# A hybrid encoder block on one core: the two channel chunks of a group take turns through the long convolution, v is split two steps later, and the tap rows move to the queue of the weights

## The chip, the cores and the metric

One core of a Trainium2 chip runs the whole block as one program. The metric is the device time of one execution in microseconds; a version's time is the median of its timed runs. A profiled execution (the trace) is a run of its own.

## The reference

One layer on x of 256 x 2048 float32. `w_in` makes q, k, v, r, gate inputs, the convolution branch's input u and two merge gates. One branch is gated linear attention (GLA), the other ("Hyena") is a short convolution followed by two long ones with gates. Both are projected, merged by sigmoid gates, projected again, and followed by layer norm and a squared-ReLU MLP with layer norm. The change is in the Hyena branch:

```python
uc = _short_conv(u, conv_w, conv_b)          # 3 taps along the sequence, per channel, plus bias
v, x1, x2 = jnp.split(uc, 3, axis=-1)
z = v
for o, gate in enumerate((x1, x2)):
    zf = jnp.fft.rfft(z, n=2 * L, axis=1)
    zc = jnp.fft.irfft(zf * filt_f[None, :, o], n=2 * L, axis=1)[:, :L]
    z = gate * (zc + skip[o] * z)
```

## The kernel before

**Products and weights.** Every large product is made of three matmuls of reduced float32: the operand's high part (a rounding copy on ScalarE, ACT, line 84) and low part (a subtraction on VectorE, DVE, line 85) are multiplied as high x high, high x low and low x high. Weights come in 300 blocks of 1 MB: `fetch` (92) loads a block into one of three `raw` buffers on SyncE's queue (SP), two blocks ahead of its use, and splits it in two halves `whi`, `wlo`, each with three buffers. TensorE (PE) thus needs a fresh `whi` from ACT and a fresh `wlo` from DVE for every half block. `token_group` (208) computes 512 output columns for all 256 tokens from four blocks, 24 matmuls each (lines 204 to 206), into two PSUM tiles, one for each 128 tokens.

**Steps.** After each block `pump` advances a clock. `later(d, fn)` puts a piece of side work on the list for d steps later; pieces that fall on the same step run in the order in which they were registered. So side work is interleaved with weight blocks at a granularity of one block. All of this is the order in which the program is written; a scheduler then places the instructions of each engine from it and from its own estimate of when each can start, so that one may move ahead of another. Each engine executes its list strictly in order, GpSimd (POOL) and SP with their DMAs too.

**The stage of the change.** Four times (s = 0 to 3) it runs the token groups v, x1, x2 (`u` columns) and `go` (GLA's output projection): 16 blocks a turn. Each of the first three is followed by `short_conv` (704): DVE multiplies the PSUM with three tap rows into `past`, `ahead` and `y` (line 708: six products of 128 x 512) and adds the bias row (709). Then four DMAs on POOL add `past`, shifted down one token, and `ahead`, shifted up one token, to `y` (716; two large ones of 508 KB and two of one row). They add to the same `y`, so each large one waits for the other. `past`, `ahead` and the four tap rows exist once (`conv_sb`): the next group overwrites them. `load_taps` (701) loads the next tap rows, a broadcast of one row to 128 partitions (1 MB).

**The long convolution.** `hy_v` splits v into `vh` and `vl`. For each 256-channel chunk c of the two in a group, and each order o: `hy_fwd` (732) loads the filter's transform `Tl` and makes two forward transforms on PE (`Zp`, six matmuls), which ACT copies to `Z`; `hy_mul` (745) multiplies on DVE (`Z` sum, `pa`, `pb`, two combinations, one more sum) and splits the result (`Yh`, `Yl`); `hy_inv` (765) transforms back (`yp`, six matmuls), multiplies with the gate x1 or x2 (`zf`) and either splits the result for o = 1 (`zh`, `zl`) or transposes it (`yT`) and stores it. Counted from the end of the v group, hy_v is at step 3; chunk 0 is at steps 5 (forward, product), 9 (inverse), 10, 14; chunk 1 at 13, 17, 18, 22. The buffers `Tl`, `Z`, `pa`, `pb`, `zh`, `zl` exist once. `reload` (824) later reads stored results back into buffers that are free by then.

Of the kernel before, what the change touches and what calls it, by code (L numbers as in the profile page):

```python
# [9 lines left out]
F32 = mybir.dt.float32  # L10
# [6 lines left out]
P = 128  # L17
D = 2048
L = 256
NT = L // P  # L20
# [22 lines left out]
def block_kernel(  # L43
# [24 lines left out]
    nc = tc.nc  # L68
    MM = nc.tensor.matmul
# [43 lines left out]
    def later(d, fn):  # L113
        clock[1] += 1
        side.append((clock[0] + d, clock[1], fn))
# [215 lines left out]

    nc.vector.memset(ones_sb, 1.0)

    def mm3(ps, lh, ll, rh, rl, start, stop):
        MM(ps, lh, rl, start=start, stop=False)
        MM(ps, lh, rh, start=False, stop=False)
        MM(ps, ll, rh, start=False, stop=stop)

# [360 lines left out]
    past, ahead = (conv_sb[:, 2 + i].rearrange("p (t d) -> p t d", t=NT) for i in range(2))  # L699

    def load_taps(i):
        nc.gpsimd.dma_start(conv_sb[:, 0:2].rearrange("p a b -> p (a b)"), conv_rows[i:i + 1, :].broadcast_to([P, 2048]))

    def short_conv(pss, i, tag, name):
        y = hp.tile([P, NT, 512], F32, tag=tag, name=name)
        for tb in range(NT):
            for j, dst in ((0, past), (2, ahead), (1, y)):
                nc.vector.tensor_tensor(dst[:, tb], pss[tb], taps[:, j], op=ALU.mult)
        nc.vector.tensor_tensor(y, y, taps[:, 3:4].broadcast_to([P, NT, 512]), op=ALU.add)
        for dst, src in (  # L710
            (y[1:P], past[0:P - 1]),
            (y[0:1, 1], past[P - 1:P, 0]),
            (y[0:P - 1], ahead[1:P]),
            (y[P - 1:P, 0], ahead[0:1, 1]),
        ):
            nc.gpsimd.dma_start(dst, src, accum_op=ALU.add)
        if i + 1 < 12:
            load_taps(i + 1)
        return y

    def hy_v(s):
        def run():
            z = tuple(hp.tile([P, NT, 512], F32R, tag=t, name=f"{t}{s}") for t in ("vh", "vl"))
            split_hi_lo(z[0], z[1], cst.pop(("v", s)))
            for i in range(2):
                cst[("z", 2 * s + i, 0)] = tuple(t[:, :, i * CW:(i + 1) * CW] for t in z)
        return run
# [1 line left out]
    def gate_part(n, c):  # L729
        return cst[(n, c // 2)][:, :, c % 2 * CW:(c % 2 + 1) * CW]  # L730

    def hy_fwd(c, o):
        def run():
            t = hp.tile([P, 2, 3, CW], F32, tag="Tl", name=f"Tl{c}{o}")
            nc.gpsimd.dma_start(t, T_dram[(c, o)])
            zh, zl = cst.pop(("z", c, o))
            z = hp.tile([P, 3, 2, CW], F32, tag="Z", name=f"Z{c}{o}")
            for ri in range(2):
                pz = psum_side(f"Zp{c}{o}{ri}")
                mm3(pz.rearrange("p (a b) -> p a b", a=2), dfth[:, ri], dftl[:, ri], zh, zl, True, True)  # L740
                nc.scalar.copy(z[:, 2:0:-1, ri, :], pz.rearrange("p (a b) -> p a b", a=2))
            cst[("Z", c, o)] = (t, z)
        return run

    def hy_mul(c, o):
        def run():
            t, z = cst.pop(("Z", c, o))
            a = hp.tile([P, 3, 2, CW], F32, tag="pa", name=f"pa{c}{o}")
            b = hp.tile([P, 3, 2, CW], F32, tag="pb", name=f"pb{c}{o}")
            TT = nc.vector.tensor_tensor  # L750
            full = [P, 3, 2, CW]
            TT(z[:, 0], z[:, 1], z[:, 2], op=ALU.add)
            TT(a, z, t[:, 0, :, None, :].broadcast_to(full), op=ALU.mult)
            TT(b, z[:, :, ::-1, :], t[:, 1, :, None, :].broadcast_to(full), op=ALU.mult)
            TT(a[:, :, 0], a[:, :, 0], b[:, :, 0], op=ALU.subtract)
            TT(a[:, :, 1], a[:, :, 1], b[:, :, 1], op=ALU.add)
            y = a[:, 1:3]
            TT(y, y, a[:, 0:1].broadcast_to([P, 2, 2, CW]), op=ALU.add)
            yh = hp.tile([P, 2, 2, CW], F32R, tag="pb", name=f"Yh{c}{o}")
            yl = hp.tile([P, 2, 2, CW], F32R, tag="Yl", name=f"Yl{c}{o}")  # L760
            split_hi_lo(yh, yl, y)
            cst[("Y", c, o)] = (yh, yl)
        return run

    def hy_inv(c, o):
        def run():
            yh, yl = cst.pop(("Y", c, o))
            py = psum_side(f"yp{c}{o}")
            py3 = py.rearrange("p (a b) -> p a b", a=2)
            mm3(py3, dfth[:, 2], dftl[:, 2], yh[:, :, 0], yl[:, :, 0], True, False)  # L770
            mm3(py3, dfth[:, 3], dftl[:, 3], yh[:, :, 1], yl[:, :, 1], False, True)
            zf = hp.tile([P, NT, CW], F32, tag="zf", name=f"zf{c}{o}")
            nc.vector.tensor_tensor(zf, py3, gate_part(("x1", "x2")[o], c), op=ALU.mult)
# [31 lines left out]
    for s in range(NCH // 2):  # L805
        for k, n in enumerate(("v", "x1", "x2")):
            pss = token_group(xT, f"u{n}{s}")
            cst[(n, s)] = short_conv(pss, 3 * s + k, n, f"c{n}{s}")
            if k == 0:
                later(3, hy_v(s))  # L810
                for i in range(2):
                    c, d = 2 * s + i, 5 + 8 * i
                    later(d, hy_fwd(c, 0))
                    later(d, hy_mul(c, 0))
                    later(d + 4, hy_inv(c, 0))
                    later(d + 5, hy_fwd(c, 1))
                    later(d + 5, hy_mul(c, 1))
                    later(d + 9, hy_inv(c, 1))
        gla_o_group()


# [1 line left out]

    def reload(c):
        def run():
            yr = hp.tile([P, 2, L], F32, tag=("v", "x1")[c % 2], name=f"yr{c}")
            nc.gpsimd.dma_start(yr, yh_dram[c])
            split_hi_lo(yhT[:, 2 * c:2 * c + 2, 0], yhT[:, 2 * c:2 * c + 2, 1], yr)
        return run
# [421 lines left out]
```

## Time and profile before

| | |
|---|---|
| timed runs | 1901.42, 1903.06, 1907.38 us; median 1903.06 |
| the profiled execution | 1907.28 us, its span (first to last instruction) 1905.3 us |
| busy | PE 1853.6, PEld 1553.2, DVE 1284.3, ACT 893.8, POOL 76.2 us |
| mean granted PE clock | 0.987 |
| weight loads | 300 of 1 MB; 399 MB in all, 210 GB/s over the span |
| first `v` product to last `go` product | 457.5 to about 909 us |

PEld is PE's weight load, which overlaps the matmuls. In a waits row, "PE go L205 <- DVE wlo L85: 24.6, 4, 7.6" means that PE stood idle ahead of line 205 until DVE's line 85 was done, for 24.6 us in total, 4 times, at most 7.6 us. In a time line, a row has start, duration, engine, line, operation and, in brackets, the idle time before it and what ended it. DMA rows tell the time from issue to landing.

### The profile page before, as it was taken

The numbers are of one execution on the slowest core, as the hardware profiler recorded it, in microseconds if no ns is written. First come the engines' busy times: TensorE is split into PE (matmuls) and PEld (weight loads), VectorE is DVE, ScalarE is ACT, GpSimd is POOL, SyncE is SP. The second block draws the span as 40 slices with busy tenths as digits, with TensorE's granted clock in tenths as the row PEclk, the third lists the DMA queues.
The fourth block names the chain that finished last, engine by engine and source line by source line (L and its number), as shares of the span: only waits on it lengthen the run. The fifth ranks groups of instructions, "written<-read, shape, count | busy, mean of one in ns | idle before, by whom it ended". The sixth has DMA issues, their size and how long they took to land.

```text
span 1905.3 us, 22925 instructions
## 1 busy us (share of the span) xinstructions
PE 1853.6 (97%) x8999; PEld 1553.2 (82%) x8999; DVE 1284.3 (67%) x1578; ACT 893.8 (47%) x1160; POOL 76.2 (4%) x116
## 2 busy tenths in 40 slices
PE   9999999999999898888999999999999999999999
PEld 7888888888777686666888889888888888888887
DVE  6878968664777786777865667666545655565557
ACT  6555658764344343333544445444434443444332
POOL 0000000000101101111000000000000000000000
PEclk9999999999999999988999999999999999999999
DMA  8667755345787877777655574555555545555553
GB/s 318 219 234 279 256 208 188 133 169 211 224 275 226 228 233 221 230 217 220 229 190 197 179 296 177 199 209 190 188 189 197 196 180 199 199 178 198 191 186 131
DMA packets 65117, 399.43 MB, mean 210 GB/s; under 512 B 8009, under 2 KB 10457, under 8 KB 24305
## 3 DMA queue, kind: packets, MB, share of 16 engines
q1 hardware_dynamic: 46080, 324.03, 47.2%
q0 software_dynamic: 11872, 54.14, 10.5%
q10 hardware_dynamic: 7056, 19.80, 2.9%
q8 instruction: 71, 1.16, 0.2%
q14 instruction: 38, 0.30, 0.0%
HBM read 369.15 MB, written 16.25 MB: 202 GB/s over the span
## 4 chain that ended last, share of the span: by engine, by line
PE 76%; DMA 8%; DVE 7%; issue 6%; ACT 1%; POOL 1%; SPq 0%; DVEq 0%; POOLq 0%; ACTq 0%
PE f L145 12%; PE f L149 6%; PE w L205 6%; PE w L206 6%; PE w L204 6%; DMA cx<-conv_sb 4%; DMA cv<-conv_sb 4%; PE g L205 3%; PE g L206 3%; PE g L204 3%; DVE wlo L85 2%; PE ho L205 2%; PE ho L204 2%; PE ho L206 2%; PE go L205 1%
## 5 line engine op out<-in xcount | busy, mean ns | idle before, releaser
L85 DVE TENSOR_TENSOR wlo<-raw,whi 128x1024 fp32r<-128x1024 f32 x584 | 711.4, 1222 | 373.7 <-ACT whi L84 371.8
L84 ACT CAST whi<-raw 128x1024 fp32r<-128x1024 f32 x584 | 614.1, 1055 | 599.4 <-PE w L206 187.9
L145 PE MATMUL f<-hT,whi 128*128 128x512 f32 x984 | 235.1, 391 | 0.0
L145 PEld LDWEIGHTS f<-hT,whi 128*128 128x128 f32 x984 | 180.8, 188 | 35.0
L205 PE MATMUL w<-wlo,f 128*128 128x512 f32 x480 | 186.7, 389 | 0.0
L206 PE MATMUL w<-whi,f 128*128 128x512 f32 x480 | 186.7, 389 | 0.0
L204 PE MATMUL w<-whi,f 128*128 128x512 f32 x480 | 167.4, 389 | 0.0
L149 PEld LDWEIGHTS f<-hT,wlo 128*128 128x128 f32 x984 | 126.2, 191 | 4.8
L149 PE MATMUL f<-hT,wlo 128*128 128x256 f32 x984 | 127.7, 283 | 0.0
L205 PE MATMUL ux<-wlo,xT 128*128 128x512 f32 x256 | 103.5, 404 | 7.3 <-DVE wlo L85 7.1
L204 PEld LDWEIGHTS w<-whi,f 128*128 128x128 f32 x480 | 90.1, 188 | 18.7
L205 PEld LDWEIGHTS w<-wlo,f 128*128 128x128 f32 x480 | 90.1, 188 | 18.7
L206 PEld LDWEIGHTS w<-whi,f 128*128 128x128 f32 x480 | 90.1, 188 | 18.6
L206 PE MATMUL ux<-whi,xT 128*128 128x512 f32 x256 | 101.9, 398 | 0.0
L157 ACT ACTIVATE f_l<-f 128x256 f32<-128x256 f32 x64 | 24.7, 385 | 162.1 <-PE f L145 159.3
L205 PE MATMUL g<-wlo,xT 128*128 128x512 f32 x256 | 100.1, 391 | 0.7 <-DVE wlo L85 0.7
L206 PE MATMUL g<-whi,xT 128*128 128x512 f32 x256 | 99.8, 390 | 0.0
L158 DVE SCALAR_TENSOR_TENSOR f_s<-f,f_l 128x256 f32<-128x256 f32 x64 | 27.2, 425 | 105.2 <-ACT f_l L157 105.2
L204 PE MATMUL ux<-whi,xT 128*128 128x512 f32 x256 | 92.6, 396 | 4.6 <-ACT whi L84 2.9
L204 PE MATMUL g<-whi,xT 128*128 128x512 f32 x256 | 93.1, 390 | 0.0
L205 PE MATMUL go<-wlo,yg 128*128 128x512 f32 x128 | 53.8, 421 | 24.6 <-DVE wlo L85 24.6
L205 PEld LDWEIGHTS ux<-wlo,xT 128*128 128x128 f32 x256 | 49.4, 193 | 22.9 <-DVE wlo L85 12.8
(431 smaller groups left out, 3232.1 us busy)
## 6 DMA issues: line engine op xcount, KB each, us to landing
raw<-wblk SPq DMA_DIRECT2D x300, 1024.0 KB, 4.8
Td<-T POOLq DMA_DIRECT2D x16, 768.0 KB, 5.0
conv_sb<-conv_rows POOLq DMA_DIRECT2D x12, 1024.0 KB, 13.0
Tl<-Td POOLq DMA_DIRECT2D x16, 768.0 KB, 4.8
w<-w4s ACTq DMA_DIRECT2D x16, 512.0 KB, 4.9
cx<-conv_sb POOLq DMA_DIRECT2D x16, 508.0 KB, 8.2
xw<-first SPq DMA_DIRECT2D x5, 896.0 KB, 12.9
zr<-ln_rows ACTq DMA_DIRECT2D x4, 1024.0 KB, 9.3
```

The source lines that it names most:

```text
L84: return (nc.scalar.copy(hi, src), nc.vector.tensor_tensor(lo, src, hi.bitcast(F32), op=ALU.subtract))
L85: nc.vector.tensor_tensor(lo, src, hi.bitcast(F32), op=ALU.subtract))
L145: MM(ps[:, :, ts], hi[:, js], act[:, kt, :, ts], start=(kt == 0 and opens), stop=(kt == KT - 1))
L149: MM(ps[:, 0, ts], lo[:, js], act[:, kt, 0, ts], start=False, stop=False)
L157: nc.scalar.activation(low, ps[:, 1], AF.Copy, scale=scale)
L158: nc.vector.scalar_tensor_tensor(dst, ps[:, 0], scale, low, op0=ALU.mult, op1=ALU.add)
L204: MM(pss[tb], sh, wh, start=(kt == 0), stop=False)
L205: MM(pss[tb], sh, wl, start=False, stop=False)
L206: MM(pss[tb], sl, wh, start=False, stop=(kt == KT - 1))
```

## The change

- The two chunks of a group alternate, one every four blocks: (chunk 0, o = 0), (chunk 1, o = 0), (chunk 0, o = 1), (chunk 1, o = 1) at steps 7, 11, 15, 19 for forward transform and product, and four steps later for the inverse. On a common step the order is forward, inverse of the one before, product.
- `hy_v` is at step 5 instead of 3.
- `Tl` is loaded in a step of its own, one step ahead of the transform.
- `hold`: the first matmul of each forward transform keeps its written place among PE's instructions.
- `load_taps` is issued on SP, the queue of the weights, two steps after the convolution, instead of on POOL at once.
- The short convolution's six products go by tap (past, y, ahead) instead of by token tile.
- `reload` uses the buffer of `vh` instead of that of x1.

```diff
+        ins = MM(ps, lh, rl, start=start, stop=False)
+        if hold:
+            tc.keep_in_program_order(ins)
...
     def load_taps(i):
-        nc.gpsimd.dma_start(conv_sb[:, 0:2]..., conv_rows[i:i + 1, :].broadcast_to([P, 2048]))
+        nc.sync.dma_start(conv_sb[:, 0:2]..., conv_rows[i:i + 1, :].broadcast_to([P, 2048]))
...
-        for tb in range(NT):
-            for j, dst in ((0, past), (2, ahead), (1, y)):
+        for j, dst in ((0, past), (1, y), (2, ahead)):
+            for tb in range(NT):
                 nc.vector.tensor_tensor(dst[:, tb], pss[tb], taps[:, j], op=ALU.mult)
...
         if i + 1 < 12:
-            load_taps(i + 1)
+            later(2, lambda: load_taps(i + 1))
...
+    def hy_load(c, o):
+        def run():
+            t = hp.tile([P, 2, 3, CW], F32, tag="Tl", name=f"Tl{c}{o}")
+            nc.gpsimd.dma_start(t, T_dram[(c, o)])
+            cst[("T", c, o)] = t
+        return run
...
-                later(3, hy_v(s))
-                for i in range(2):
-                    c, d = 2 * s + i, 5 + 8 * i
-                    later(d, hy_fwd(c, 0))
-                    later(d, hy_mul(c, 0))
-                    later(d + 4, hy_inv(c, 0))
-                    later(d + 5, hy_fwd(c, 1))
-                    later(d + 5, hy_mul(c, 1))
-                    later(d + 9, hy_inv(c, 1))
+                later(5, hy_v(s))
+                steps = [(2 * s + j % 2, j // 2, 4 * j) for j in range(4)]
+                for c, o, d in steps:
+                    later(6 + d, hy_load(c, o))
+                    later(7 + d, hy_fwd(c, o))
+                for c, o, d in steps:
+                    later(11 + d, hy_inv(c, o))
+                for c, o, d in steps:
+                    later(7 + d, hy_mul(c, o))
...
-            yr = hp.tile([P, 2, L], F32, tag=("v", "x1")[c % 2], name=f"yr{c}")
+            yr = hp.tile([P, 2, L], F32, tag=("v", "vh")[c % 2], name=f"yr{c}")
```

What it does to the order of the instructions, at three places of the second turn (s = 1; numbers behind the names only tell buffers' tiles apart). First DVE's list around the end of the v group, before (`pb` closes with its sums ahead of the convolution's products, two `wlo` between them):

```order
L754 TENSOR_TENSOR pb_4986<-Z_4974,Tl_4972 128x1536
L773 TENSOR_TENSOR zf_5038<-yp_5031,cx_4745 128x512
L755 TENSOR_TENSOR pa_4985<-pa_4985,pb_4986 128x3x256
L756 TENSOR_TENSOR pa_4985<-pa_4985,pb_4986 128x3x256
L85 TENSOR_TENSOR wlo_0_5052<-raw_5049,whi_0_5051 128x1024
L758 TENSOR_TENSOR pa_4985<-pa_4985 128x1024
L85 TENSOR_TENSOR wlo_1_5056<-raw_5049,whi_1_5055 128x1024
L708 TENSOR_TENSOR conv_sb<-uv_0_4936,conv_sb 128x512 x2
```

and the same place after the change:

```order
L762 TENSOR_TENSOR pb_5067<-Z_5042,Tl_5006 128x1536
L85 TENSOR_TENSOR zl_5063<-zf_5060,zh_5062 128x512
L85 TENSOR_TENSOR wlo_1_5015<-raw_5008,whi_1_5014 128x1024
L763 TENSOR_TENSOR pa_5066<-pa_5066,pb_5067 128x3x256
L764 TENSOR_TENSOR pa_5066<-pa_5066,pb_5067 128x3x256
L710 TENSOR_TENSOR conv_sb<-uv_0_4936,conv_sb 128x512
L710 TENSOR_TENSOR cv_5112<-uv_0_4936,conv_sb 128x512
L710 TENSOR_TENSOR conv_sb<-uv_0_4936,conv_sb 128x512
L710 TENSOR_TENSOR conv_sb<-uv_1_4937,conv_sb 128x512
L710 TENSOR_TENSOR cv_5112<-uv_1_4937,conv_sb 128x512
L710 TENSOR_TENSOR conv_sb<-uv_1_4937,conv_sb 128x512
L85 TENSOR_TENSOR wlo_0_5081<-raw_5078,whi_0_5080 128x1024
```

The complex product now stands directly ahead of the convolution's six products, with one `wlo` between `pb` and the first of them and none between them. (`zf`, `pa` and a `wlo` stand ahead of these rows.)

Second, DVE's list at the split of v (`vl`), before, ahead of x1's products (`cx` is x1's `y`):

```order
L754 TENSOR_TENSOR pb_5227<-Z_5215,Tl_5213 128x1536
L85 TENSOR_TENSOR wlo_0_5241<-raw_5238,whi_0_5240 128x1024
L85 TENSOR_TENSOR vl_5273<-cv_5117,vh_5272 128x1024
L85 TENSOR_TENSOR wlo_1_5245<-raw_5238,whi_1_5244 128x1024
L755 TENSOR_TENSOR pa_5226<-pa_5226,pb_5227 128x3x256
L756 TENSOR_TENSOR pa_5226<-pa_5226,pb_5227 128x3x256
L708 TENSOR_TENSOR conv_sb<-ux_0_5130,conv_sb 128x512 x2
```

and after:

```order
L710 TENSOR_TENSOR conv_sb<-ux_0_5124,conv_sb 128x512
L710 TENSOR_TENSOR conv_sb<-ux_1_5125,conv_sb 128x512
L85 TENSOR_TENSOR wlo_0_5275<-raw_5272,whi_0_5274 128x1024
L766 TENSOR_TENSOR pa_5260<-pa_5260 128x1024
L85 TENSOR_TENSOR vl_5355<-cv_5112,vh_5354 128x1024
L85 TENSOR_TENSOR wlo_1_5279<-raw_5272,whi_1_5278 128x1024
L711 TENSOR_TENSOR cx_5306<-cx_5306,conv_sb 128x1024
```

The split of v has moved behind x1's products, about a block and a half later in DVE's list.

Third, POOL's list at the third v group, before:

```order
L735 DMA Tl_5972<-Td_1332 128x1536
L790 DMA yd_5806<-yo_5804 128x512
L716 DMA cv_5876<-conv_sb 127x1024
L716 DMA cv_5876<-conv_sb 1x16x32
L702 DMA conv_sb<-conv_rows 128x2048
L716 DMA cv_5876<-conv_sb 1x16x32
L716 DMA cv_5876<-conv_sb 127x1024
L735 DMA Tl_6118<-Td_1500 128x1536
```

and after:

```order
L737 DMA Tl_5765<-Td_1158 128x1536
L737 DMA Tl_5953<-Td_1332 128x1536
L718 DMA cv_5871<-conv_sb 127x1024
L718 DMA cv_5871<-conv_sb 1x16x32 x2
L718 DMA cv_5871<-conv_sb 127x1024
L737 DMA Tl_6151<-Td_1500 128x1536
```

The load of the tap rows has left the adding DMAs' queue. It is now in SP's list between two weight loads, behind the second group's v:

```order
L98 DMA raw_5126<-wblk 128x2048
L98 DMA raw_5160<-wblk 128x2048
L98 DMA raw_5197<-wblk 128x2048
L704 DMA conv_sb<-conv_rows 128x2048
L98 DMA raw_5272<-wblk 128x2048
L98 DMA raw_5320<-wblk 128x2048
```

More of the change, by code (lines that the diff above doesn't have):

```diff
@@ L332, in block_kernel, with mm3 @@
     nc.vector.memset(ones_sb, 1.0)
-    def mm3(ps, lh, ll, rh, rl, start, stop):
-        MM(ps, lh, rl, start=start, stop=False)
+    def mm3(ps, lh, ll, rh, rl, start, stop, hold=False):
+        ins = MM(ps, lh, rl, start=start, stop=False)
+        if hold:
+            tc.keep_in_program_order(ins)
         MM(ps, lh, rh, start=False, stop=False)
@@ L701, in load_taps @@
     def load_taps(i):
-        nc.gpsimd.dma_start(conv_sb[:, 0:2].rearrange("p a b -> p (a b)"), conv_rows[i:i + 1, :].broadcast_to([P, 2048]))
+        nc.sync.dma_start(conv_sb[:, 0:2].rearrange("p a b -> p (a b)"), conv_rows[i:i + 1, :].broadcast_to([P, 2048]))
     def short_conv(pss, i, tag, name):
         y = hp.tile([P, NT, 512], F32, tag=tag, name=name)
-        for tb in range(NT):
-            for j, dst in ((0, past), (2, ahead), (1, y)):
+        for j, dst in ((0, past), (1, y), (2, ahead)):
+            for tb in range(NT):
                 nc.vector.tensor_tensor(dst[:, tb], pss[tb], taps[:, j], op=ALU.mult)
@@ L730, in gate_part @@
         return cst[(n, c // 2)][:, :, c % 2 * CW:(c % 2 + 1) * CW]
-    def hy_fwd(c, o):
+    def hy_load(c, o):
         def run():
@@ L735, in run, with hy_fwd @@
             nc.gpsimd.dma_start(t, T_dram[(c, o)])
+            cst[("T", c, o)] = t
+        return run
+    def hy_fwd(c, o):
+        def run():
+            t = cst.pop(("T", c, o))
             zh, zl = cst.pop(("z", c, o))
@@ L739, in run @@
                 pz = psum_side(f"Zp{c}{o}{ri}")
-                mm3(pz.rearrange("p (a b) -> p a b", a=2), dfth[:, ri], dftl[:, ri], zh, zl, True, True)
+                mm3(pz.rearrange("p (a b) -> p a b", a=2), dfth[:, ri], dftl[:, ri], zh, zl, True, True, hold=True)
                 nc.scalar.copy(z[:, 2:0:-1, ri, :], pz.rearrange("p (a b) -> p a b", a=2))
```

## The prediction

> **What bounds the kernel now.** I read the clock and busy times by stage first, then who waits for whom inside the stage that stood out, then the time lines of TensorE (PE), VectorE (DVE), ScalarE (ACT) and the DMA queues around its longest waits. The busy times of three stretches (columns: length, PE, PEld, DVE, ACT, POOL busy, granted clock, DMA share, GB/s):
>
> ```profile
> 457.30:912.00 454.70, 410.42 (x1736) 331.67 (x1735) 335.77 (x338) 175.68 (x190) 58.24 (x79) 0.95 0.75 230
> 0.00:457.00 457.00, 454.57 (x2232) 377.62 (x2233) 345.63 (x554) 282.24 (x462) 14.16 (x30) 1.00 0.62 223
> 912.00:1905.00 993.00, 988.31 (x5033) 843.70 (x5031) 602.58 (x687) 435.64 (x508) 3.84 (x7) 1.00 0.54 194
> ```
>
> PE is busy all the time except from 457 to 912 us, which is the changed stage: sixteen token groups (v, x1, x2 of the convolution branch, then the output projection `go`, four times). There 454.7 - 410.4 = 44 us are idle, and only there does the clock fall below 1.00. The waits of PE in that stage (us in total, times, longest):
>
> ```profile
> PE go L205 <- DVE wlo L85: 24.6, 4, 7.6
> PE Zp L335 <- DVE vl L85: 7.8, 2, 3.9
> PE ux L205 <- DVE wlo L85: 7.1, 7, 2.4
> PE ux L204 <- ACT whi L84: 2.9, 1, 2.9
> PE ux L204 <- DMA raw<-wblk: 1.7, 1, 1.7
> ```
>
> and, of the other engines in the same stretch:
>
> ```profile
> ACT vh L84 <- DMA cv<-conv_sb: 34.3, 4, 9.9
> ...
> DVE vl L85 <- ACT vh L84: 24.1, 3, 9.7
> ...
> DVE conv_sb L708 <- DMA cx<-conv_sb: 18.5, 4, 5.6
> ...
> DVE conv_sb L708 <- DMA conv_sb<-conv_rows: 4.0, 2, 2.2
> ```
>
> PE waits for weight halves (`wlo`), and DVE and ACT, which make them in order, stand behind a DMA. There are two places in a group. The first is where x2's multiplication overwrites `past` and `ahead`:
>
> ```profile
> 742.73 1.68 POOL L716 DMA_DIRECT2D cx<-conv_sb  x2 [9.88 <-DVE cx L709]
> 743.80 1.21 POOL L702 DMA_DIRECT2D conv_sb<-conv_rows  x1
> 750.00 1.65 POOL L716 DMA_DIRECT2D cx<-conv_sb  x2 [5.00 <-DMA cx<-conv_sb]
> ...
> 758.15 0.69 DVE L708 TENSOR_TENSOR conv_sb<-ux,conv_sb 128x512 f32<-128x512 f32 x1 [1.88 <-DMA conv_sb<-conv_rows]
> 763.51 1.89 DVE L708 TENSOR_TENSOR conv_sb<-ux,conv_sb 128x512 f32<-128x512 f32 x3 [4.67 <-DMA cx<-conv_sb]
> ...
> 769.51 0.79 PE L205 MATMUL go<-wlo,yg 128*128 128x512 f32 x1 [7.43 <-DVE wlo L85]
> 770.10 0.63 PE L206 MATMUL go<-whi,yg 128*128 128x512 f32 x1
> 770.53 0.63 PE L205 MATMUL go<-wlo,yg 128*128 128x512 f32 x1
> ```
>
> x1's adding DMAs run from 742.73 to 763.51, 20.8 us, in two legs (7.3, then 13.5), with the taps load of 743.80 in the same queue. DVE waits 1.88 for the taps and 4.67 for `ahead`; PE loses 7.43, and then its matmuls stand 0.43 us apart. The second place is the split of v (`hy_v`), which stands behind v's own adding DMAs:
>
> ```profile
> 725.60 1.05 ACT L84 CAST vh<-cv 128x1024 fp32r<-128x1024 f32 x1 [9.87 <-DMA cv<-conv_sb]
> 726.68 1.22 DVE L85 TENSOR_TENSOR vl<-cv,vh 128x1024 fp32r<-128x1024 f32 x1 [9.69 <-ACT vh L84]
> 728.05 0.47 PE L335 MATMUL Zp<-vl,dfth 128*128 128x512 f32 x1 [3.93 <-DVE vl L85]
> ```
>
> **What can be won at most.** The pace of PE undisturbed:
>
> ```profile
> 479.04 0.39 PE L206 MATMUL uv<-whi,xT 128*128 128x512 f32 x1
> 479.26 0.62 PE L204 MATMUL ux<-whi,xT 128*128 128x512 f32 x2
> ...
> 481.98 0.62 PE L204 MATMUL ux<-whi,xT 128*128 128x512 f32 x2
> ```
>
> One half block (12 matmuls) takes 481.98 - 479.26 = 2.72 us, so 0.227 a matmul and 5.44 a block. After the long stall the spacing is 0.43, for some 8 matmuls: 8 x 0.2 = 1.6 us, call it 1.7 for each stall of 2 us or more. There are eight of those (four of `go`, two of `Zp`, the 2.4 and the 2.9): 14 us. So 44 + 14 = 58 us is all that removing every stall could give.
>
> **Part by part.** *Split of v at step 5 instead of 3, first transform at 7 instead of 5.* The chain after v's psum is: DVE work up to L709, then the DMAs. Now the split is asked for 3 x 5.44 = 16 us after the psum and waits 9.9 us, so the data is there at about 26 to 29 us. In the new order `vl` stands behind x1's multiplications, at least 4 x 5.44 + 2.7 (the transform's 12 matmuls) + 3.6 = 28 us after the psum, in front of it ACT's `vh`. The 9.9 us stall falls to between 0 and 1; I take 0.
>
> *Taps off GpSimd's queue, multiplication by past, y, ahead.* `ahead` is now overwritten late among the six products, and between the adding DMAs of a group nothing else stands in GpSimd's queue. The DMA issues of the stage (KB each, median us to landing), then three rows of the page, then the spread for `raw` in the stage:
>
> ```profile
> raw<-wblk SPq DMA_DIRECT2D x65, 1024.0 KB, 7.1
> conv_sb<-conv_rows POOLq DMA_DIRECT2D x11, 1024.0 KB, 13.0
> ```
>
> ```profile
> L84 ACT CAST whi<-raw 128x1024 fp32r<-128x1024 f32 x584 | 614.1, 1055 | 599.4 <-PE w L206 187.9
> ...
> Tl<-Td POOLq DMA_DIRECT2D x16, 768.0 KB, 4.8
> ...
> zr<-ln_rows ACTq DMA_DIRECT2D x4, 1024.0 KB, 9.3
> ```
>
> ```profile
> DMA to landing us min/median/max: 4.7/7.1/14.5
> ```
>
> The new load is bounded by 9.3 us (a broadcast of the same size on another engine's queue) and 13.0 (the same load today); I take 9.3. The second leg of the adding chain lies between 7.3 (the first leg) and 13.5 (today); I take 10. By the walk below, where t = 0 is PE's end of v's third block, the bias addition is done at 18.5 and the chain at 36 (39.3 if it is as long as today); x1's first product over `ahead` comes at 25.9 + 12.3 = 38.2. DVE's waits of 18.5 us for `cx` go; at worst 1.1 us stays at a group. `load_taps` waits on SP for DVE's bias addition, and behind it on SP stand the weight loads. The taps have landed at 18.5 + 9.3 = 27.8 (31.5 at worst). The next weight load is issued when DVE has made the half before, at 21.9; wholly behind the taps it lands at 34.9 (38.6). ACT wants it when PE begins the half two before it: 25.9 + 8.2 = 34.1, and PE misses it only 3.2 us later (a half is wanted 2 x 2.72 + 0.23 after its buffer is free, and takes ACT 1.06 and DVE 1.22 with some 0.2 between). Cost 0 to 1.3 us for each of 11 loads, that is 0 to 14; I take 0. The cover is the depth of three weight buffers; without it, 11 x 9.3.
>
> [...]
>
> *Chunks take turns, a step every four blocks.* Work on PE, DVE and ACT is the same: the same matmuls, products and splits, 16 `Tl` loads. What changes is that each of DVE's complex products now stands one block ahead of a group's end and meets the short convolution there. The durations of these pieces, start to start:
>
> ```profile
> 690.21 1.23 DVE L85 TENSOR_TENSOR wlo<-raw,whi 128x1024 fp32r<-128x1024 f32 x1 [1.37 <-ACT whi L84]
> 691.35 1.75 DVE L754 TENSOR_TENSOR pb<-Z,Tl 128x1536 f32<-128x1536 f32 x1
> 693.02 0.68 DVE L773 TENSOR_TENSOR zf<-yp,cx 128x512 f32<-128x512 f32 x1
> 693.62 0.95 DVE L755 TENSOR_TENSOR pa<-pa,pb 128x768 f32<-128x768 f32 x1
> 694.48 0.95 DVE L756 TENSOR_TENSOR pa<-pa,pb 128x768 f32<-128x768 f32 x1
> 695.35 1.22 DVE L85 TENSOR_TENSOR wlo<-raw,whi 128x1024 fp32r<-128x1024 f32 x1
> 696.49 1.28 DVE L708 TENSOR_TENSOR conv_sb<-uv,conv_sb 128x512 f32<-128x512 f32 x2
> ```
>
> That is 1.67 for each of `pa` and `pb`, 0.87 for each sum, 0.60 for each 512-wide product, 1.14 for a `wlo`. Walk through the new row of DVE (shown with the change), t = 0 when PE ends v's third block. PE does 12 transform matmuls to 2.72, v's last block to 8.16, x1's first to 13.60, then wants `wlo_0_5081` at 13.8. DVE: one `wlo` to 2.3, `Z` and `zf` (behind PE's 2.72) to 3.6, `pa`, `pb` to 7.0, `zl` 7.6, `wlo_1_5015` 8.7, two sums 10.4, six products 14.0, `wlo_0_5081` 15.2. PE stalls 1.4 us. The next three operations are as wide as a `wlo`; the third, the bias addition, ends at 18.5. With three more `wlo` by 23 DVE is level again. At x1 the same walk gives 0.9 and, behind `vl`, 0.7; at x2, where four products stand behind `pa` and `pb`, 2.0. The first group has it at x2 only, three further groups at v, x1 and x2: ten meetings at 1.6 us, 16 us; I add 1 for the first x1, whose products stand at once behind v's chain, and 4 for half clock behind the four at x2, which reach 2 us: 21 us. Bounds: 0 (the pieces happen to fit) and 10 x (4 + 1.7) = 57, if the backlog does not drain between meetings.
>
> *Tl loads as a step of their own, `hold`, `reload` into vh's buffer.* The load is issued a step earlier; in GpSimd's new row each follows at once on the last chain that it could stand behind, a block (5.44 us) ahead of its use, against 4.8 us to land. `hold` keeps PE from meeting a transform ahead of its data. `vh` is last read at step 11, before the g2 groups begin. I take nothing for the three; a `Tl` that is late by a microsecond holds DVE at `pa`, ahead of a `wlo`, and is inside the bounds of those ten meetings.
>
> **Sum.** 58 - 21 = 37 us less. The profiled execution took 1907.3 us (span 1905.3); the median of the three timed runs is 1903.1, so 1866 us by the median (1870 if taken like the profiled one). With the remaining stalls between 8 and 36 us, this case spans 1853 to 1881.
>
> **Rivals.** *All stalls go* (1845): if the pieces on DVE interleave better than in my walk, for instance because PE itself comes late. For it: in the rows above two `wlo` come 695.35 - 690.21 = 5.1 us apart, and none of PE's stalls of 2 us or more is there. Against: the walk has two such gaps in a row, of 6.4 and 6.5 us, against 2.72 us a half.
>
> *No change* (about 1902): DVE becomes the bound. An interval of four blocks is 4 x 5.44 + 2.7 = 24.5 us of PE, and holds 8 `wlo` (9.1), a complex product with its split (8.0), `zf` and `zl` (1.2), the convolution (4.7) and at x1 `vl` (1.1): 23 to 24 us. The point is 24.5; any DVE wait of a microsecond, on the chain or the taps, carries over, and the 57 us above eat the 58.
>
> *Slower* (1940): weights starve behind the taps. The place is SP's queue, where the weight load stands behind the taps at every one of 11 convolutions. If the load takes the 14.5 us that is the longest today, it lands at 42.3, 42.3 - 34.1 - 3.2 = 5.0 us late at PE, plus 1.7 for the clock: 11 x 6.7 = 74, and 1903 - 58 + 21 + 74 = 1940. It decides from 37 / 11 = 3.4 us a load on. Against: the same bytes cross the DMA engines today, at a mean share of 0.75. [...]
>
> **Chances.** Forecast 0.71, all stalls gone 0.13, no change 0.08, slower 0.08. That is 0.84 for faster by over 0.3% (about what a measurement of this kernel can tell from none), 0.08 within, 0.08 slower. The range, 1846 to 1890, takes in the forecast's span, the floor but for a microsecond, and part of the way to no change.
>
> **What would show it.** In the stage from 457 us: PE's waits add to 10 to 30 us instead of 44, in ten pieces of 1 to 2 us, released by `wlo` at the first blocks of x1, x2 and `go`; none of 7 us at `go`, none at `Zp`; `vh` waits under 1 us; DVE's multiplication does not wait for `cx`; the clock in the stage 0.98 or more. Wrong would be: long waits of `whi` for `raw` behind each taps load (the slower case), DVE without idle time in the stage and stalls over 3 us at every group (no change), or the `cx` waits still there, which would say that the taps were not what made the chain long.

## The result, and the profile after

The changed kernel took 1878.7 us, the median of four runs (1874.1 to 1882.8), beside 1905.2 us for the kernel before in the same measurement (1901.4 to 1909.4): a ratio of 0.986, 95% interval 0.9825 to 0.9894. That is 26.5 us less. The forecast was 37 less, 1866 us, with a range from 1846 to 1890.

The profiled execution after took 1882.8 us, its span 1881.0. Here is its busy time from the first `v` product to the last `go` product (the columns are those of the prediction's first fence):

```profile
460.30:885.40 425.10, 401.28 (x1724) 326.47 (x1723) 335.38 (x336) 174.00 (x188) 52.71 (x70) 0.97 0.79 244
```

and of the kernel before between the same two instructions:

```profile
457.50:909.60 452.10, 407.82 (x1724) 329.53 (x1723) 333.43 (x335) 173.80 (x188) 58.24 (x79) 0.95 0.75 229
```

The stage is 27.0 us shorter. It begins 2.8 us later and ends 24.2 us earlier, and the span is 24.3 us shorter. PE's idle time in it fell from 44.3 to 23.8 us, and the clock rose from 0.95 to 0.97. (The stage begins at 460 instead of 457 us; in the profiles of all the kernels below, which are the same up to there, it begins anywhere between 456 and 461.) Who waits for whom in it, after:

```profile
ACT vh L84 <- DMA cv<-conv_sb: 15.4, 4, 6.7
PE go L205 <- DVE wlo L85: 13.7, 4, 4.7
...
PE ux L205 <- DVE wlo L85: 7.6, 9, 2.5
DVE conv_sb L710 <- DMA cx<-conv_sb: 7.1, 3, 3.0
DVE conv_sb L710 <- DMA cv<-conv_sb: 4.5, 3, 4.0
ACT whi L84 <- DMA raw<-wblk: 4.3, 1, 4.3
...
PE ux L204 <- ACT whi L84: 2.5, 1, 2.5
```

(Waits are named below by the convolution at which DVE or ACT falls behind. PE meets a wait "at x1" in the first two blocks of the next group, x2, and one "at x2" in those of `go`; `ux` stands for the products of x1 and x2 alike.)

No row for `Zp` is left: PE no longer waits for the split of v there. The waits of `go` were 24.6 us and are 13.7. But DVE still waits for `cx`, which the prediction had named as a sign against it. The place, in the second turn, shows why. These are x1's adding DMAs, the taps load, x2's products over `ahead`, the next `wlo` and the product of `go` that waits for it:

```profile
623.04 1.72 POOL L718 DMA_DIRECT2D cx<-conv_sb  x2 [4.78 <-DVE cx L711]
634.54 1.63 POOL L718 DMA_DIRECT2D cx<-conv_sb  x2 [9.78 <-DMA cx<-conv_sb]
...
622.77 0.33 SPq L704 DMA_DIRECT2D conv_sb<-conv_rows  x1
...
644.76 1.29 DVE L710 TENSOR_TENSOR conv_sb<-ux,conv_sb 128x512 f32<-128x512 f32 x2 [2.42 <-DMA cx<-conv_sb]
...
647.16 2.35 DVE L85 TENSOR_TENSOR wlo<-raw,whi 128x1024 fp32r<-128x1024 f32 x2
...
648.43 0.79 PE L205 MATMUL go<-wlo,yg 128*128 128x512 f32 x1 [4.18 <-DVE wlo L85]
```

The chain runs from 623.04 to 644.76, 21.7 us. Before it was 20.8. Its first leg went from 7.3 to 11.5 us, since the taps load leaves SP in the same moment (622.77); the second went from 13.5 to 10.2. The load lands sooner (8.9 us in the median, 13.0 before), as the DMA issues say, and the weights land about as before (7.6 and 7.1):

```profile
raw<-wblk SPq DMA_DIRECT2D x65, 1024.0 KB, 7.6
conv_sb<-conv_rows SPq DMA_DIRECT2D x11, 1024.0 KB, 8.9
```

At the split of v in the same turn ACT waits 3.2 us, and PE next to nothing behind it. The first row below is the meeting at the end of the v group, the second the half block behind the split:

```profile
592.65 0.50 PE L205 MATMUL ux<-wlo,xT 128*128 128x512 f32 x1 [1.08 <-DVE wlo L85]
...
618.25 0.50 PE L205 MATMUL ux<-wlo,xT 128*128 128x512 f32 x1 [0.31 <-DVE wlo L85]
...
615.86 1.05 ACT L84 CAST vh<-cv 128x1024 fp32r<-128x1024 f32 x1 [3.21 <-DMA cv<-conv_sb]
```

The third and fourth turns are like this one. In the first, `vh` stands where it stood before in ACT's list, behind the same weight cast; ACT waits 6.7 us for v there, and PE 2.5 us twice behind it:

```profile
509.91 1.04 ACT L84 CAST vh<-cv 128x1024 fp32r<-128x1024 f32 x1 [6.70 <-DMA cv<-conv_sb]
511.95 0.73 PE L204 MATMUL ux<-whi,xT 128*128 128x512 f32 x2 [2.52 <-ACT whi L84]
515.19 0.80 PE L205 MATMUL ux<-wlo,xT 128*128 128x512 f32 x1 [2.50 <-DVE wlo L85]
```

### The profile page after: what moved, and what is told of

Its sections match the earlier page's. It is cut to its first block, busy times and chain, and to the rows that moved or that the text cites. A ratio compares the mean times of both kernels' runs of the same rounds, so it can differ in the third digit from the quotient of the medians.

```text
span 1881.0 us, 22915 instructions
## 1 busy us (share of the span) xinstructions
PE 1846.8 (98%) x8999; PEld 1549.6 (82%) x8999; DVE 1284.3 (68%) x1578; ACT 891.3 (47%) x1160; POOL 69.3 (4%) x104
## 4 chain that ended last, share of the span: by engine, by line
PE 77%; DMA 8%; DVE 7%; issue 6%; ACT 1%; POOL 0%; SPq 0%; DVEq 0%; ACTq 0%; POOLq 0%
PE f L145 12%; PE f L149 6%; PE w L206 6%; PE w L204 6%; PE w L205 6%; DMA cx<-conv_sb 3%; DMA cv<-conv_sb 3%; PE g L205 3%; PE g L206 3%; PE g L204 3%; DVE wlo L85 2%; PE ho L206 2%; PE ho L205 2%; PE ho L204 2%; PE v L204 1%
## 5 line engine op out<-in xcount | busy, mean ns | idle before, releaser
L157 ACT ACTIVATE f_l<-f 128x256 f32<-128x256 f32 x64 | 24.6, 384 | 162.3 <-PE f L145 159.4
L205 PEld LDWEIGHTS ux<-wlo,xT 128*128 128x128 f32 x256 | 48.7, 190 | 21.7 <-DVE wlo L85 11.8
L205 PE MATMUL go<-wlo,yg 128*128 128x512 f32 x128 | 53.0, 414 | 13.7 <-DVE wlo L85 13.7
```

Of the source, the lines that this page charges most:

```text
L157: nc.scalar.activation(low, ps[:, 1], AF.Copy, scale=scale)
L205: MM(pss[tb], sh, wl, start=False, stop=False)
```

## The experiments

The first theory, from this comparison, was A: most of the gain is the split of v, and the taps load, which shares the DMA engines with the adding chain (they are busy for 0.99 of the 8.7 us, 623.04 to 631.70, in which both are under way in the second turn), keeps the rest. Its rival, B, was the prediction's own account of the taps.

**1. The taps alone.** The kernel before with the three edits on the taps, the old steps kept:

```diff
-        nc.gpsimd.dma_start(conv_sb[:, 0:2]..., conv_rows[i:i + 1, :].broadcast_to([P, 2048]))
+        nc.sync.dma_start(conv_sb[:, 0:2]..., conv_rows[i:i + 1, :].broadcast_to([P, 2048]))
...
-        for tb in range(NT):
-            for j, dst in ((0, past), (2, ahead), (1, y)):
+        for j, dst in ((0, past), (1, y), (2, ahead)):
+            for tb in range(NT):
...
-            load_taps(i + 1)
+            later(2, lambda: load_taps(i + 1))
```

> The kernel before, with only the taps load moved to SP two steps later and the products taken by tap; hy_v stays at step 3 and the chunks keep their old order. Theory A (the taps load still shares the DMA engines with the adding chain, so the chain stays near 21 us; the v stalls come from where hy_v stands): the stalls of 3.9 us at Zp stay, the four waits of go stay above 4 us, gain 3 to 8 us against before, ratio 0.996 to 0.998. Theory B (the taps' place in GpSimd's queue made the chain long): the chain falls to about 15 us, DVE no longer waits for cx, the waits of go fall to about 2 us each, gain 25 to 31 us, ratio 0.984 to 0.987.

Measured: 1880.5 us, ratio 0.9865 (0.9845 to 0.9884). That is B's number, and all of the gain: the new steps and the later split add nothing to the three edits that these intervals could tell. But B's reason isn't there: DVE waits 12.0 us for `cx` (18.5 before), and a first leg takes 11.7 us. Nor did the waits at `Zp` stay, as A expected: 2.4 of the 7.8 us are left.

**2. The turns alone.** The changed kernel with those three edits undone:

```diff
-        nc.sync.dma_start(conv_sb[:, 0:2]..., conv_rows[i:i + 1, :].broadcast_to([P, 2048]))
+        nc.gpsimd.dma_start(conv_sb[:, 0:2]..., conv_rows[i:i + 1, :].broadcast_to([P, 2048]))
...
-        for j, dst in ((0, past), (1, y), (2, ahead)):
-            for tb in range(NT):
+        for tb in range(NT):
+            for j, dst in ((0, past), (2, ahead), (1, y)):
...
-            later(2, lambda: load_taps(i + 1))
+            load_taps(i + 1)
```

> The changed kernel with the taps load back on GpSimd's queue at once and the products in the old order; the split at step 5 and the chunks' turns stay. Theory A (most of the gain is the split of v, 19 us of idle time and some 7 us of clock; the taps' move gives little): 1880 to 1890 us, ratio to before 0.987 to 0.992, the waits of vh for v's chain a few us, none at Zp; the waits of go near 6 us each. Theory B (the taps' move carries the gain): 1895 to 1903 us, ratio 0.995 to 1.00, with waits of go above 7 us.

Measured: 1917.5 us, ratio 1.0061 (1.0038 to 1.0084): slower than before, which neither theory had. The time line of ACT and PE in the second turn:

```profile
619.28 1.04 ACT L84 CAST vh<-cv 128x1024 fp32r<-128x1024 f32 x1 [12.28 <-DMA cv<-conv_sb]
...
621.33 1.22 PE L204 MATMUL ux<-whi,xT 128*128 128x512 f32 x2 [5.00 <-ACT whi L84]
...
661.38 0.80 PE L205 MATMUL go<-wlo,yg 128*128 128x512 f32 x1 [6.90 <-DVE wlo L85]
```

The split of v, at the same step 5, costs PE 5.0 us here (3.2 and 3.8 in the next turns), and `go` waits 6.9 us. ACT's lists tell the difference. With the taps on POOL:

```
L84 CAST whi88_1_5167<-raw88_5161 128x1024
L84 CAST whi89_0_5199<-raw89_5197 128x1024
L749 COPY Z11_5231<-Zp110_5232 128x2x256
L749 COPY Z11_5231<-Zp111_5237 128x2x256
L84 CAST vh1_5355<-cv1_5112 128x1024
L84 CAST whi89_1_5203<-raw89_5197 128x1024
L84 CAST whi90_0_5274<-raw90_5272 128x1024
```

In the changed kernel `vh1` stands behind `whi89_1` and `whi90_0`, two weight casts later. The step does not decide it: with step 6 written instead of 5 the list with the taps on POOL is the same here. Of the three edits it is the queue alone. With the load on SP `vh1` stands behind `whi90_0`, and with the load on POOL ahead of `whi89_1`, in either order of the products and whether the load is issued at once or two steps later. The likely way is the scheduler's estimate of when v's data is there, which a load in the adding DMAs' queue changes; the estimate itself is not on record. So edits that look independent were not.

**3. The side work one step later.** In the changed kernel:

```diff
-                    later(6 + d, hy_load(c, o))
-                    later(7 + d, hy_fwd(c, o))
+                    later(7 + d, hy_load(c, o))
+                    later(8 + d, hy_fwd(c, o))
...
-                    later(11 + d, hy_inv(c, o))
+                    later(12 + d, hy_inv(c, o))
...
-                    later(7 + d, hy_mul(c, o))
+                    later(8 + d, hy_mul(c, o))
```

> The changed kernel with every load, transform, product and inverse of the chunks one step later, so that DVE's complex product no longer meets the short convolution at a group's end. Theory A (the waits left at go are DVE standing at the products over ahead behind the adding chain): the waits of wlo of about 1.1 us at the first blocks of x1 and the 0.3 to 0.4 us inside it go, together some 5 us; the waits at go stay at 3 us or more, since the products over ahead now come earlier and wait for cx longer: 1872 to 1880 us. Theory B (the waits left are the burst of complex product and convolution): nearly all waits go, go included, the stage has under 8 us of idle time and the clock is 0.99 or more: 1852 to 1860 us.

Measured: 1880.2 us, ratio 0.9869 (0.9842 to 0.9895). The waits of `go` behind their `wlo` went altogether, against A, but PE's waits at the `ux` products are 21 us instead of 10, all of them at x1: the time only moved.

**4. Without the later taps loads.**

```diff
-        if i + 1 < 12:
-            later(2, lambda: load_taps(i + 1))
```

> The changed kernel without the eleven later loads of the taps: all convolutions take the first row's taps, the loads are left out, every other instruction stays. Theory A (the taps load lengthens the first leg of the adding chain from 7.3 to 11.5 us): the first leg falls to 7 to 8 us, the chain to 15 to 18 us, DVE does not wait for cx, the waits of go fall from 3.5 to 4.7 us to about 2.0 us: 1864 to 1872 us. Theory B (the chain is as long by itself, or DVE's burst makes the waits): waits of go stay at 3.5 us or more, 1876 to 1882 us.

Measured: 1887.8 us, ratio 0.9906 (0.989 to 0.9922): 9 us *slower* than with the loads. The waits of `go` did fall, to 8.0 us in all, and the first legs to 7.1 to 7.8 us, as A says; but the waits at the `ux` products rose to 21.4 us. ACT's list has `vh` two weight casts earlier again, as in experiment 2. So neither 2 nor 4 was the comparison that it was meant to be. For the runs that follow the split was held where a run had to have it, by a helper that puts ACT's cast behind a named weight cast:

```diff
+            casts[n, h] = split_hi_lo(hi, lo, raw[:, h * 1024:(h + 1) * 1024])[0]
-            split_hi_lo(hi, lo, raw[:, h * 1024:(h + 1) * 1024])
...
+            with tc.issue_after(casts[(fetched[0] - 2, 0) if s else (fetched[0] - 3, 1)].ins):
+                split_hi_lo(z[0], z[1], cst.pop(("v", s)))
-            split_hi_lo(z[0], z[1], cst.pop(("v", s)))
```

With this the lists of PE and ACT are those of the changed kernel in experiments 6 to 9, and DVE's differ only in where products of the convolution stand (in 6 one `wlo` a turn stands elsewhere too). The new theory, C: what counts is where the products and the split stand in the lists of DVE and ACT; D: it is the queue after all.

**5. The order of the products alone**, in the kernel before:

```diff
-        for tb in range(NT):
-            for j, dst in ((0, past), (2, ahead), (1, y)):
+        for j, dst in ((0, past), (1, y), (2, ahead)):
+            for tb in range(NT):
```

> The kernel before with one edit: the six products of a convolution are taken by tap, past, y, ahead, instead of by token half; the taps stay on GpSimd's queue. Theory C (the gain of the taps edit is the order on DVE: with the products over ahead last, fewer products stand behind the wait for the adding chain): the waits of go fall from about 7.5 us to 5.5 us, gain 5 to 9 us, ratio 0.995 to 0.9975. Theory D (the queue makes the gain): within 0.2 per cent of before.

Measured: 1889.0 us, ratio 0.9913 (0.9893 to 0.9932): 16.7 us, some twice what C expected, with the taps still in POOL's queue. The place in the third turn that the prediction showed of before:

```profile
752.64 1.29 DVE L708 TENSOR_TENSOR conv_sb<-ux,conv_sb 128x512 f32<-128x512 f32 x2 [1.95 <-DMA cx<-conv_sb]
...
755.12 0.55 PE L205 MATMUL go<-wlo,yg 128*128 128x512 f32 x1 [2.74 <-DVE wlo L85]
```

DVE waits 1.95 us instead of 4.67, since four of the products now come ahead of the wait, and only 1.2 us of work stands between the wait's end and the next `wlo` (752.64 to 753.85; before it was 4.7, from 763.51 to the `wlo` at 768.24). PE waits 2.74 us instead of 7.43. C had counted only the products; two sums of the complex product moved ahead with them. The split was not held here: in the second turn `vh1` stands one weight cast later in ACT's list than before, and a wait of PE for `whi` there, 2.85 us before, is gone. So the 16.7 us are not the order's alone; in the third turn, shown here, the lists of ACT and PE are those of before.

**6. The turns, with the split held in place.** Experiment 2 with the helper.

> As turns_only (the changed kernel with the taps back on GpSimd's queue at once and the old order of the products), but the split of v is held at the place that it has in the changed kernel, behind two more weight casts on ACT. Theory C (turns_only lost because the split of v stood two weight casts earlier than in the changed kernel, in front of weights that PE then waited for): the waits of x1's second block, 3.2 to 5.0 us of whi and some 2 us of wlo a group, fall to under 1 us, 1895 to 1902 us. Theory D (the queue is what counts): 1910 us or more.

Measured: 1898.6 us, ratio 0.9962 (0.9943 to 0.9982), 18.9 less than experiment 2. That is the worth of two places in ACT's list, with DVE's `vl` moving along (and a few instructions late in the fourth turn). The waits for `whi` in the last three turns are gone, which PE had in x2's first block and not, as the expectation says, in x1's second. But C's "under 1 us" was missed: 2.2 to 3.6 us a turn are left for `wlo` in its second, where DVE had waited for v's chain, and `go` still waits 5.1, 6.8 and 7.9 us. DVE's row at x2 in the third turn, and PE's wait:

```profile
756.90 0.69 DVE L711 TENSOR_TENSOR conv_sb<-ux,conv_sb 128x512 f32<-128x512 f32 x1 [5.02 <-DMA cx<-conv_sb]
757.51 1.75 DVE L763 TENSOR_TENSOR pa<-Z,Tl 128x1536 f32<-128x1536 f32 x1
759.17 1.75 DVE L764 TENSOR_TENSOR pb<-Z,Tl 128x1536 f32<-128x1536 f32 x1
...
763.23 2.35 DVE L85 TENSOR_TENSOR wlo<-raw,whi 128x1024 fp32r<-128x1024 f32 x2
...
764.51 0.79 PE L206 MATMUL go<-wlo,yg 128*128 128x512 f32 x1 [6.79 <-DVE wlo L85]
```

The product over `ahead` is the second of the six here, and behind it stand `pa`, `pb` and four more products: 6.3 us (756.90 to 763.23) from the wait's end to the next `wlo`. In the changed kernel, whose order puts a product over y in between, `pa` and `pb` come ahead of the wait, and these are 2.4 us (644.76 to 647.16).

**7. The changed kernel, the taps back on POOL at once**, product order and split as in the changed kernel:

```diff
-        nc.sync.dma_start(conv_sb[:, 0:2]..., conv_rows[i:i + 1, :].broadcast_to([P, 2048]))
+        nc.gpsimd.dma_start(conv_sb[:, 0:2]..., conv_rows[i:i + 1, :].broadcast_to([P, 2048]))
...
-            later(2, lambda: load_taps(i + 1))
+            load_taps(i + 1)
```

> The changed kernel with one edit: the taps load is back on GpSimd's queue at once; order of the products and place of the split of v as in the changed kernel. Theory C (the queue itself is worth little): 1880 to 1888 us, waits of go 3.5 to 5.5 us. Theory D (the queue is what counts): 1895 us or more, with waits of go near 7 us and DVE waiting for the taps.

Measured: 1879.0 us, ratio 0.9859 (0.9838 to 0.9881). The changed kernel has 0.986 (0.9825 to 0.9894). With the lists held, the move to the weights' queue is worth nothing in the sum, a little less even than C expected (and the waits of `go` are 1.7 to 2.6 us, not its 3.5 to 5.5); the order of the products, 1898.6 to 1879.0, is worth 19.6: in the third turn `go` waits 1.67 us instead of 6.79. The time line of the second turn says how the same sum comes about:

```profile
597.17 1.71 POOL L719 DMA_DIRECT2D cv<-conv_sb  x2 [11.33 <-ACT whi L84]
598.27 1.20 POOL L705 DMA_DIRECT2D conv_sb<-conv_rows  x1
604.92 1.65 POOL L719 DMA_DIRECT2D cv<-conv_sb  x2 [5.45 <-DMA cv<-conv_sb]
...
617.83 1.29 DVE L711 TENSOR_TENSOR conv_sb<-ux,conv_sb 128x512 f32<-128x512 f32 x2 [2.91 <-DMA cv<-conv_sb]
...
621.50 0.50 PE L206 MATMUL ux<-wlo,xT 128*128 128x512 f32 x1 [2.98 <-DVE wlo L85]
...
649.34 0.50 PE L206 MATMUL go<-wlo,yg 128*128 128x512 f32 x1 [1.89 <-DVE wlo L85]
```

With the load behind the first two adding DMAs the first leg is 7.8 us, and the chain 20.7. Here it is x1 that waits for v's chain, 3.0 us, and `go` only 1.9; in the changed kernel it is the other way round, 0.3 and 4.2.

**8. Without the later taps loads, the split held in place.** Experiment 4 with the helper.

> As no_reload (the changed kernel without the eleven later loads of the taps, all convolutions take the first row's taps), but the split of v is held at the place that it has in the changed kernel. Theory A (the taps load stretches the adding chain from about 15 to 21 us, and no_reload lost only because its split of v had moved two weight casts forward): the first leg 7 to 8 us, x1's second block without waits over 1 us, waits of go 2 us or less: 1866 to 1873 us. Rival (the load costs nothing): 1877 to 1881 us.

Measured: 1863.3 us, ratio 0.9781 (0.9766 to 0.9797): A, as far as the load goes, and somewhat below its range. The stage, and the second turn at x2, with DVE's first product over `ahead`:

```profile
456.90:865.10 408.20, 394.10 (x1724) 321.35 (x1723) 334.64 (x336) 173.70 (x188) 52.62 (x70) 1.00 0.75 225
```

```profile
615.91 1.72 POOL L719 DMA_DIRECT2D cx<-conv_sb  x2 [6.77 <-DVE cx L712]
623.28 1.63 POOL L719 DMA_DIRECT2D cx<-conv_sb  x2 [5.65 <-DMA cx<-conv_sb]
...
635.08 1.28 DVE L711 TENSOR_TENSOR conv_sb<-ux,conv_sb 128x512 f32<-128x512 f32 x2
...
614.52 0.50 PE L206 MATMUL ux<-wlo,xT 128*128 128x512 f32 x1 [0.39 <-DVE wlo L85]
638.75 0.51 PE L206 MATMUL go<-wlo,yg 128*128 128x512 f32 x1 [1.67 <-DVE wlo L85]
```

PE is idle for 14.1 us and the clock is 1.00. DVE doesn't wait for the chain 19.2 us after its start; in the changed kernel the chain needs 21.7. The difference looks small, but it stands ahead of `wlo`: PE's wait is 1.67 instead of 4.18. A's chain of 15 us isn't there: the last of its four transfers left at 623.8 and took 9.4 us to land, which makes the chain 17.3 us.

**9. `ahead` of x2 in a buffer of its own.** The loads stay; x2's products over `ahead` go to the buffer of v's convolution, which is free once v is split:

```diff
+        nxt = hp.tile([P, NT, 512], F32, tag="v", name=f"nx{i}") if i % 3 == 2 else ahead
-        for j, dst in ((0, past), (1, y), (2, ahead)):
+        for j, dst in ((0, past), (1, y), (2, nxt)):
...
-            (y[0:P - 1], ahead[1:P]),
-            (y[P - 1:P, 0], ahead[0:1, 1]),
+            (y[0:P - 1], nxt[1:P]),
+            (y[P - 1:P, 0], nxt[0:1, 1]),
```

> The changed kernel, with x2's products over ahead written into the buffer of v's convolution, which is free by then, so that they don't wait for x1's adding chain; the taps load and its place stay, and the split of v is held at its place. Theory A (the waits of go are the products over ahead behind a chain that the taps load stretches to 21 us): DVE's waits for cx go, the waits of go fall from 4.2, 4.7 and 3.5 to 1.7 to 2.0 us as without the load, the chain stays at 21 us: 1865 to 1871 us. Rival (something else of the load holds the weights at go): waits of go above 3 us, 1876 to 1881 us.

Measured: 1868.7 us, ratio 0.9798 (0.9784 to 0.9812). The first leg is as long as in the changed kernel, and nobody waits for it:

```profile
624.36 1.72 POOL L720 DMA_DIRECT2D cx<-conv_sb  x2 [4.87 <-DVE cx L713]
635.55 1.63 POOL L720 DMA_DIRECT2D cx<-conv_sb  x2 [9.46 <-DMA cx<-conv_sb]
...
643.53 0.69 DVE L712 TENSOR_TENSOR nx<-ux,conv_sb 128x512 f32<-128x512 f32 x1
...
647.20 0.50 PE L206 MATMUL go<-wlo,yg 128*128 128x512 f32 x1 [1.67 <-DVE wlo L85]
```

So some 10 of the 15.4 us that the loads cost come from this one wait, give or take several, since the four runs of the changed kernel lie 8.7 us apart; the rest was not taken apart.

**10. One step later, the split held in place.** Experiment 3 with the helper: ACT's `vh` two weight casts later than there.

> As shift1 (every load, transform, product and inverse one step later), with the split of v held two weight casts later, at the place that it has in the changed kernel. Theory C (the waits of 1.5 and 3.3 us a group in shift1 are weights behind the split of v that stands too early, in front of x1's products): they fall under 1 us each, 1864 to 1872 us. Rival (they are the complex product meeting x1's convolution, which only moved by a step): they stay, 1877 to 1882 us.

Measured: 1862.6 us, ratio 0.977 (0.9757 to 0.9783), the fastest of all: 44.5 us less than before in this measurement (1907.2), and some 16 less than the changed kernel. In experiment 3 one turn had these two waits at x1:

```profile
613.52 0.50 PE L205 MATMUL ux<-wlo,xT 128*128 128x512 f32 x1 [1.48 <-DVE wlo L85]
620.33 0.50 PE L205 MATMUL ux<-wlo,xT 128*128 128x512 f32 x1 [3.32 <-DVE wlo L85]
```

and here the same turn has these, in a stage with 11.6 us of idle time:

```profile
456.30:860.50 404.20, 392.64 (x1714) 320.14 (x1714) 330.95 (x332) 170.77 (x185) 51.89 (x68) 0.99 0.81 253
```

```profile
615.16 0.50 PE L206 MATMUL ux<-wlo,xT 128*128 128x512 f32 x1 [0.35 <-DVE wlo L85]
619.64 0.50 PE L206 MATMUL ux<-wlo,xT 128*128 128x512 f32 x1 [1.46 <-DVE wlo L85]
```

The larger wait is 1.46 us here, not under 1 as C expected. The split is not all that changed between 3 and 10: with it the scheduler also moved products and inverse transforms at x2 and `go` of the last three turns in PE's list. So how much of the 17.6 us between them is the split's stays open.

(The stages of 3 and 10 hold fewer of the transforms' matmuls than the others, since some now lie behind the last `go`.)

## Why the prediction was right, and where it was wrong

**The result as a sum of parts.** From before to experiment 2, the steps alone: 12.2 us more. To 6, the place of the split: 18.9 less. To 7, the order of the products: 19.6 less. To the changed kernel, the queue: 0.3 less. Together, but for rounding, that is the 26.5 less that were measured, as it must be, since each part starts where the one before ends. Along another way the parts are others: on the old steps the three edits on the taps gave 24.7 by themselves (experiment 1), and the move of the load to SP is also what put the split in its better place. The prediction had the sign and most of the size, but put them on other parts; that the sum came so near is in part luck.

**Split of v.** "Falls to between 0 and 1; I take 0" was right for PE in three turns of four: no wait at `Zp`, waits of at most 0.4 us at x1. The reason given, that `vl` stands behind x1's multiplications, was read from the new lists and holds in these. In the first turn `vh` and `vl` did not move, and PE still loses 5.0 us behind them (2.9 before). And the gain was put down to step 5 instead of 3, but step 5 doesn't do it: experiments 2 and 4 have it too, and wait up to 5.0 and 3.4 us at x1. ACT's waits for `vh`, forecast under 1 us, are 6.7 us in the first turn and 2.2 to 3.3 in the others, where they cost PE little.

**The step that failed: the taps.** "I take the second leg at 10 us and the chain is done at 36 (39.3 if it is as long as today)" was half a reckoning. The second leg did come to 10.2. The first was left at 7.3, with no term for the load that now starts beside it, and became 11.5. The chain got longer (21.7 and, in the third turn, 22.3), beyond the worst case in the text, and DVE's waits for `cx` stayed at 1.7 to 3.0 us. That `go` still gained came from the product order, which the prediction had mentioned in half a sentence and not priced (experiments 5 to 7); so far as it goes, the gain at `go` was luck.

**The queue of the taps.** Its worth is 0.3 us, between experiment 7 and the changed kernel. I had let one row of another place (9.3 against 13.0 us to landing) speak for a gain of the other queue. Which transfers wait does differ: the load did land in 8.9, and the chain paid for it (11.5 us in the first leg instead of 7.3). On the old steps the same move may have been worth more, 1889.0 (experiment 5) against 1880.5 (experiment 1); other instructions moved there as well, so this stays open.

**The mis-sized term: 21 us left over.** Left are 23.8 us of idle time and 7.2 us of slower matmuls (PE is busy for 401.28 us here and 394.10 in experiment 8, at the same count), 31.0 in all. (By the prediction's own sizes its ten meetings make 17 us and not 16.) The meetings of complex product and convolution were sized well: 1.4 at v, 0.9 and 0.7 at x1 and 2.0 at x2 were forecast. Measured are 1.08 at v in the changed kernel, and where no chain is in the way (experiment 8) 0.4 to 1.2 at x1 and 1.67 at x2. What was missing is the chain at x2 (13.7 us instead of 8), the split of v in the first turn (5.0 at the first x1 instead of 1), and the clock behind them (7.2 instead of 4). The other meetings, at v and x1, came out some 4 us smaller than forecast. The net 10 us are most of the 12.7 between forecast and result.

**The other terms.** The weights behind the taps cost nothing, as taken: ACT waits once for `raw`, 4.3 us, where it was 27.0 us in eight waits before, and none of PE's waits follows on it, so the slower rival fell on its first condition. No wait for `Tl` shows in the changed kernel. DVE is busy for 335 of 425 us and is not the bound; its pieces only come in bursts.

**The ceiling.** Of the 58 us named as what removing every stall could give, experiment 10 has 44.5; what is left of its stage is 11.6 us of idle time.

## What to carry to other kernels

On an engine that runs its list in order, ask of every wait what stands behind it: taking work of 3 to 4 us a turn from behind a wait to ahead of it was worth 16.7 and 19.6 us, and moving one cast by two places 18.9, while the queue of a load, with the lists held, was worth nothing in the sum. Where a scheduler places instructions by its own estimates, an edit moves others as well, so compare the lists first and hold the rest in place, or an experiment measures the side effect. A transfer that leaves one queue can still slow those left in it (here the first leg went from 7.3 to 11.5 us): look up which serial chain runs in that moment and price its legs anew, each of them.

## What the runs showed of the hardware

The clock did not go by the length of a wait alone. In experiment 1, two waits of PE of the same length:

```profile
626.26 0.79 PE L205 MATMUL ux<-wlo,xT 128*128 128x512 f32 x1 [3.05 <-DVE wlo L85]
626.85 0.63 PE L206 MATMUL ux<-whi,xT 128*128 128x512 f32 x1
...
767.73 0.50 PE L205 MATMUL go<-wlo,yg 128*128 128x512 f32 x1 [3.05 <-DVE wlo L85]
768.07 0.40 PE L206 MATMUL go<-whi,yg 128*128 128x512 f32 x1
```

Behind the first the matmuls stand 0.43 us apart for some 3 us; behind the second they go on at 0.23. (Before, at 0.43 us apart, the granted clock was 0.52, from 769.51 to 773.84; at 0.23 it was 1.00, from 774.30 to 778.00.) What sets the two waits apart, no run here shows. For a sum it means that the prediction's price of 1.7 us for each wait of 2 us or more is not a rule: the eight matmuls behind the first of these took 1.4 us more than those behind the second.

Whom a load of 1 MB slows depended on its queue, in three kernels whose lists differ in little else. Without it (experiment 8) the eleven first legs of v, x1 and x2 took 7.4 us in the median, and the weight loads between 460 and 890 us 7.3 us to land. With it on the weights' queue (the changed kernel) the legs took 11.7 us and the weights 7.6. With it on POOL's queue, behind the first two adding DMAs (experiment 7), the legs took 7.6 us and the weights 8.4.
